# Reading the moving tile of every float32r product from its last column to its first

## Chip, cores and metric

One core of one Trainium2 chip. The metric is the device time in microseconds (us) of the kernel's one launch. The time of the kernel before is the median of three runs; a separate profiled execution gives the span, the busy times and the rows below.

## What is computed

One layer of a streaming-encoder trunk on a sequence of 1024 positions of width 1024, all in float32. The layer normalises its input, projects it, mixes it in four branches (chunked attention, a gated linear recurrence, a spatial gate, a recurrent branch with a convolution), projects and gates each branch, sums them, projects the sum and adds it to the input. A second half normalises again and applies a gated feed-forward network of hidden width 2816. Cut to what matters:

```python
def hybrid_mixer(h, w_in, ..., w_branch, w_out):
    z = h @ w_in
    aq, ak, av, bq, bf, bi, bg, cu, cv, dx, dg, gates = split_in(z)
    ...
    proj = jnp.einsum('bsnw,nwd->bsnd', outs, w_branch)
    g = jax.nn.sigmoid(gates.reshape(B, S, N_BRANCH, D_MODEL))
    merged = jnp.sum(g * proj, axis=2)
    return merged @ w_out

def swiglu(h, w1, w2):
    gt, up = jnp.split(h @ w1, 2, axis=-1)
    return (jax.nn.silu(gt) * up) @ w2

def reference(x, ...):
    h = rms_norm(x, norm_mix_pre[l])
    y = hybrid_mixer(h, ...)
    x = x + rms_norm(y, norm_mix_post[l])
    h = rms_norm(x, norm_ffn_pre[l])
    x = x + rms_norm(swiglu(h, w_ffn_in[l], w_ffn_out[l]), norm_ffn_post[l])
```

The large matrix products (with `w_in`, `w_branch`, `w_out`, `w_ffn_in`, `w_ffn_out`) are where almost all of TensorE's time goes.

## The kernel before, in words

Each large float32 product is made of three products of the faster type float32r. Both operands are split into a high part (a copy rounded to float32r, ScalarE, L135) and a low part (the rest, VectorE, L136). Then high times high, high times low and low times high are added up in one PSUM bank. A TensorE product takes a stationary operand of 128 rows and 128 columns, which a weight load brings in, and streams a moving tile of 128 rows and up to 512 columns past it. Each moving column gives one PSUM column.

The three products are issued in two places. `mm3` (L208 to L212) serves everything up to the feed-forward sums: the loop runs over the k tiles and issues L210, L211 and L212 for each, all into the same PSUM tile. `gemm_cm` calls it with weights stationary and 512 tokens moving, `gemm_tm` with tokens stationary and 256 weight columns moving, two groups of which fill one PSUM tile. `wino` (seven products of half-size blocks in place of eight, with sums of blocks made beforehand by `column_sums` and `token_sums`) calls it through its own `prod`. The local `step` of `ffn_out` (L1225 to L1230) issues the same three products for the last large multiplication, on units of which columns 0 to 511 are stationary and 512 to 1023 are moving.

Four steps of the order of work bear on the change. The tiles of PSUM come from one pool of eight banks, `pp` (L54): a new tile takes the bank of the tile that was released longest ago, so a product that opens a tile may have to wait for those who used the bank before. A tile framework records every dependency and puts semaphore waits on the instructions. A scheduler with a timeline model of its own sets the order in which each engine's instructions stand. And each finished tile is read once or twice from PSUM by ScalarE or VectorE in ascending column order (L340, L349, L356, L1072, L1262).

The small products of the branches (attention scores, transposes, the recurrences) are plain float32 and are issued elsewhere (L379, L541, L554, L666, L685, L698 and others). The diff does not touch them.

Of the kernel before, what the change touches and what calls it, by code (L numbers as in the profile page):

```python
# [38 lines left out]
def hybrid_trunk(ctx, tc, x, w_in, w_branch, w_out, w_ffn_in, w_ffn_out, cols, gpost, gfpost,  # L39
                 abias, wst, bsr, wabd, wxbd, lvl, tril, eye, out, dbg=None):  # L40
    nc = tc.nc
# [164 lines left out]

    def mm3(ps, lh, ll, rh, rl, n, more=False, ks=None):

        for k in ks or range(n):
            nc.tensor.matmul(ps, lhsT=lh(k), rhs=rh(k), start=(not more and k == 0), stop=False, skip_group_check=more)  # L210
            nc.tensor.matmul(ps, lhsT=lh(k), rhs=rl(k), start=False, stop=False, skip_group_check=more)  # L211
            nc.tensor.matmul(ps, lhsT=ll(k), rhs=rh(k), start=False, stop=(k == n - 1), skip_group_check=more)  # L212

    def gemm_cm(unit, xh, xl, fn, name, cs=slice(0, P), n=KT, fine=1):
        hi, lo = unit
        for h in range(2):
            ps = psmm(name)
            ts = slice(h * 512, (h + 1) * 512)
            for f in range(fine):
                mm3(ps, lambda k: hi[:, k, cs], lambda k: lo[:, k, cs],  # L220
                    lambda k: xh(k, ts), lambda k: xl(k, ts), n, ks=range(f * n // fine, (f + 1) * n // fine))
                if f == fine - 1:
                    fn(ps, ts)
                yield

    def gemm_tm(units, xh, xl, fn, name, tts):
        (ha, la), (hb, lb_) = units
        for tt in tts:
            ps = psmm(name)
            for u in range(2):  # L230
                ts = slice((tt + u) * P, (tt + u + 1) * P)
                mm3(ps[:, u * 256 : (u + 1) * 256], lambda k: xh(k, ts), lambda k: xl(k, ts),
                    lambda k: (ha if k < 4 else hb)[:, k % 4, :], lambda k: (la if k < 4 else lb_)[:, k % 4, :], KT)
            fn(ps, tt)
            yield
# [86 lines left out]
    def wino(ops, c0_, c1_, done):  # L322
# [11 lines left out]
        def prod(ps, un, o, b, more=False):  # L334
            mm3(ps, lambda k: un[0][:, o + k, :], lambda k: un[1][:, o + k, :], ops[b][0], ops[b][1], 4, more)
# [834 lines left out]
    def ffn_out(chunk, first, final):  # L1170
        n = len(chunk)
# [53 lines left out]
        def step(un, ps, t, start, stop, more):  # L1225
            hi, lo = un
            ts = slice(t * P, (t + 1) * P)
            nc.tensor.matmul(ps, lhsT=hi[:, ts], rhs=hi[:, 512:1024], start=start, stop=False, skip_group_check=more)  # L1228
            nc.tensor.matmul(ps, lhsT=hi[:, ts], rhs=lo[:, 512:1024], start=False, stop=False, skip_group_check=more)  # L1229
            nc.tensor.matmul(ps, lhsT=lo[:, ts], rhs=hi[:, 512:1024], start=False, stop=stop, skip_group_check=more)  # L1230

        n_prod = [0]

        def prod(pst, A, B, evac, more=False, after=None):

            n_prod[0] += 1
            if not final:
                for i, q in enumerate(pairs_):
                    u = units(q, A, B)
                    for t in range(4):  # L1240
                        step(u, pst[t], t, not more and i == 0, i == n - 1, more)
                        if i == n - 1:
                            evac(t, pst[t])
                    if after:
                        after(q)
                return

            un = [units(q, A, B, n_prod[0] in (2, 4, 6, 7)) for q in pairs_]
            for q in pairs_ if after else ():
                after(q)  # L1250
            for t in range(4):
                for i in range(n):
                    step(un[i], pst[t], t, not more and i == 0, i == n - 1, more)
                evac(t, pst[t])
# [133 lines left out]
```

## Time and profile before

| what | value |
|---|---|
| median of three runs | 1612.23 us (1610.47 to 1612.44) |
| profiled execution: its own time | 1611.69 us |
| profiled execution: span from first to last instruction | 1609.9 us |
| TensorE (PE) busy | 1535.5 us, 95% of the span |
| VectorE (DVE) busy | 1059.6 us, 66% |
| GpSimd (POOL) busy | 607.1 us, 38% |
| ScalarE (ACT) busy | 571.7 us, 36% |
| mean granted TensorE clock | 0.986 of 2.4 GHz |

In the profile a product stands as a MATMUL on PE and its weight load as an LDWEIGHTS on PEld, which overlaps PE. A product's duration runs from its start to the end of its passage through the array, so neighbours overlap: what a product costs in a dense stream is the distance between two starts, called its pitch here, and not its duration. The profiled execution took 1.8 us more than its span and lies 0.5 us below the median.

### The profile page before, as it was taken

How to read it: one execution, taken by the hardware profiler on the slowest of the kernel's cores; microseconds unless marked ns; L12 is line 12 of the kernel's file. 1: busy time of each engine (PE TensorE's matmuls, PEld its weight loads, DVE VectorE, ACT ScalarE, POOL GpSimd, SP SyncE). 2: the span in 40 equal slices, each digit the busy share in tenths (PEclk: the TensorE clock that was granted, in tenths of full speed). 3: DMA queues.
4: the chain of work that ended last, by engine and by line, in shares of the span. 5: the costliest groups of instructions: out<-in, count | busy, mean ns of one | idle time of the engine just before them, and what ended most of it. 6: DMA issues, size and time to landing. Idle time of an engine off the chain costs nothing. (4 is left out here: it accounts for less than half of the span.)

```text
span 1609.9 us, 20631 instructions
## 1 busy us (share of the span) xinstructions
PE 1535.5 (95%) x7880; PEld 1278.8 (79%) x7880; DVE 1059.6 (66%) x1415; ACT 571.7 (36%) x945; POOL 607.1 (38%) x475
## 2 busy tenths in 40 slices
PE   7899999999998999999999988999999999898986
PEld 7888888888887878776899966888888888686865
DVE  5986674444479475656766698555455556879898
ACT  6333343333322253334335533222232323343533
POOL 2665333323100101222442256533333335729194
PEclk9999999999999999999999998999999999999988
DMA  6224333333461148432325511222222236430212
GB/s 237 100 93 159 115 112 105 112 105 105 159 220 60 50 160 319 159 144 87 110 93 183 188 42 66 85 79 86 79 79 83 81 121 231 185 105 26 80 53 105
DMA packets 108547, 191.48 MB, mean 119 GB/s; under 512 B 6432, under 2 KB 65440, under 8 KB 108448
## 3 DMA queue, kind: packets, MB, share of 16 engines
q1 hardware_dynamic: 108448, 190.16, 33.9%
q8 instruction: 62, 1.02, 0.3%
q14 instruction: 37, 0.30, 0.1%
HBM read 136.66 MB, written 53.48 MB: 118 GB/s over the span
## 5 line engine op out<-in xcount | busy, mean ns | idle before, releaser
L136 DVE TENSOR_TENSOR wlo_ws<-s,whi_ws 128x1024 fp32r<-128x1024 f32 x78 | 118.2, 1515 | 51.8 <-ACT whi_ws L135 51.8
L356 DVE TENSOR_TENSOR u<-u,mm_w 128x512 f32<-128x512 f32 x39 | 26.8, 687 | 175.9 <-PE mm_w L212 175.9
L135 ACT CAST whi_ws<-s 128x1024 fp32r<-128x1024 f32 x78 | 82.2, 1054 | 157.4 <-PE mm_w L211 146.8
L1229 PE MATMUL mm_fo<-wlo_fo,whi_fo 128*128 128x512 f32 x308 | 123.7, 404 | 12.1 <-DVE wlo_fo L136 12.1
L319 POOL TENSOR_TENSOR s<-raw_pj 128x512 f32<-128x512 f32 x38 | 59.0, 1553 | 197.2 <-DMA raw_pj<-in_w_in 187.1
L1230 PE MATMUL mm_fo<-whi_fo,wlo_fo 128*128 128x512 f32 x308 | 119.4, 396 | 0.0
L319 POOL TENSOR_TENSOR s<-raw_fu 128x512 f32<-128x512 f32 x20 | 35.1, 1757 | 200.5 <-DMA raw_fu<-in_w_ffn_in 200.5
L1228 PE MATMUL mm_fo<-whi_fo 128*128 128x512 f32 x308 | 94.5, 399 | 9.3 <-ACT whi_fo L135 8.0
L136 DVE TENSOR_TENSOR wlo_fo<-af,whi_fo 128x512 fp32r<-128x512 f32 x66 | 72.9, 1112 | 26.3 <-ACT whi_fo L135 25.8
L1229 PEld LDWEIGHTS mm_fo<-wlo_fo,whi_fo 128*128 128x128 f32 x308 | 59.4, 193 | 30.7 <-DVE wlo_fo L136 18.4
L135 ACT CAST whi_fo<-af 128x512 fp32r<-128x512 f32 x66 | 40.6, 622 | 106.7 <-PE mm_fo L1230 56.0
L1228 PEld LDWEIGHTS mm_fo<-whi_fo 128*128 128x128 f32 x308 | 59.1, 192 | 23.7 <-ACT whi_fo L135 9.3
L340 ACT COPY m<-mm_w 128x512 f32<-128x512 f32 x39 | 22.9, 587 | 154.4 <-PE mm_w L212 140.7
L211 PE MATMUL mm_wo<-wlo_wo,mh 128*128 128x256 f32 x256 | 72.3, 284 | 1.9 <-DVE wlo_wo L136 1.9
L212 PE MATMUL mm_wo<-whi_wo,ml 128*128 128x256 f32 x256 | 72.4, 284 | 1.7 <-DVE ml L918 1.7
L210 PE MATMUL mm_w<-h2h,whi_wa 128*128 128x512 f32 x160 | 63.0, 394 | 10.9 <-ACT m L340 10.9
L210 PE MATMUL mm_wo<-whi_wo,mh 128*128 128x256 f32 x256 | 71.7, 284 | 0.7 <-ACT whi_wo L135 0.7
L1230 PEld LDWEIGHTS mm_fo<-whi_fo,wlo_fo 128*128 128x128 f32 x308 | 59.2, 192 | 12.1
L211 PE MATMUL mm_w<-h2l,whi_wa 128*128 128x512 f32 x160 | 62.7, 392 | 0.0
L212 PE MATMUL mm_w<-h2h,wlo_wa 128*128 128x512 f32 x160 | 62.7, 392 | 0.0
L210 PE MATMUL mm_w<-T2h,whi_ws 128*128 128x512 f32 x156 | 60.9, 390 | 0.6 <-ACT whi_ws L135 0.6
L212 PE MATMUL mm_w<-T4h,a 128*128 128x512 f32 x156 | 60.7, 389 | 0.0
(399 smaller groups left out, 4825.0 us busy)
## 6 DMA issues: line engine op xcount, KB each, us to landing
raw_pj<-in_w_in SPq DMA_DIRECT2D x19, 1024.0 KB, 6.0
gt<-st_g SPq DMA_DIRECT2D x22, 512.0 KB, 6.4
raw_fg<-in_w_ffn_in SPq DMA_DIRECT2D x11, 1024.0 KB, 4.9
raw_fu<-in_w_ffn_in SPq DMA_DIRECT2D x11, 1024.0 KB, 5.5
af<-act SPq DMA_DIRECT2D x22, 512.0 KB, 4.3
wf<-in_w_ffn_out SPq DMA_DIRECT2D x18, 512.0 KB, 6.6
xt<-in_x SPq DMA_DIRECT2D x16, 512.0 KB, 7.7
raw_wo<-in_w_out SPq DMA_DIRECT2D x8, 1024.0 KB, 5.1
```

The costliest lines, as they stand in the source:

```text
L135: nc.scalar.copy(hi, src)
L136: nc.vector.tensor_tensor(lo, src, hi.bitcast(F32), op=ALU.subtract)
L210: nc.tensor.matmul(ps, lhsT=lh(k), rhs=rh(k), start=(not more and k == 0), stop=False, skip_group_check=more)
L211: nc.tensor.matmul(ps, lhsT=lh(k), rhs=rl(k), start=False, stop=False, skip_group_check=more)
L212: nc.tensor.matmul(ps, lhsT=ll(k), rhs=rh(k), start=False, stop=(k == n - 1), skip_group_check=more)
L319: last_sum[0] = nc.gpsimd.tensor_tensor(out_, x0, x1_, op=op)
L340: nc.scalar.copy(m1, p1)
L356: nc.vector.tensor_tensor(u2, u2, p3, op=ALU.add)
L1228: nc.tensor.matmul(ps, lhsT=hi[:, ts], rhs=hi[:, 512:1024], start=start, stop=False, skip_group_check=more)
L1229: nc.tensor.matmul(ps, lhsT=hi[:, ts], rhs=lo[:, 512:1024], start=False, stop=False, skip_group_check=more)
L1230: nc.tensor.matmul(ps, lhsT=lo[:, ts], rhs=hi[:, 512:1024], start=False, stop=stop, skip_group_check=more)
```

## The change

In both places the moving tile and the PSUM tile are taken with their columns reversed (`[:, ::-1]`). The address of the first element is that of the last column, and the step along the row is -1 in place of +1, for what is read from SBUF and for what is written to PSUM alike. So column c of the moving tile still gives column c of PSUM, and the stationary operand is untouched.

```diff
     def mm3(ps, lh, ll, rh, rl, n, more=False, ks=None):
 
+        pd = ps[:, ::-1]
         for k in ks or range(n):
-            nc.tensor.matmul(ps, lhsT=lh(k), rhs=rh(k), start=(not more and k == 0), stop=False, skip_group_check=more)
-            nc.tensor.matmul(ps, lhsT=lh(k), rhs=rl(k), start=False, stop=False, skip_group_check=more)
-            nc.tensor.matmul(ps, lhsT=ll(k), rhs=rh(k), start=False, stop=(k == n - 1), skip_group_check=more)
+            h, l = rh(k)[:, ::-1], rl(k)[:, ::-1]
+            nc.tensor.matmul(pd, lhsT=lh(k), rhs=h, start=(not more and k == 0), stop=False, skip_group_check=more)
+            nc.tensor.matmul(pd, lhsT=lh(k), rhs=l, start=False, stop=False, skip_group_check=more)
+            nc.tensor.matmul(pd, lhsT=ll(k), rhs=h, start=False, stop=(k == n - 1), skip_group_check=more)
...
             ts = slice(t * P, (t + 1) * P)
-            nc.tensor.matmul(ps, lhsT=hi[:, ts], rhs=hi[:, 512:1024], start=start, stop=False, skip_group_check=more)
-            nc.tensor.matmul(ps, lhsT=hi[:, ts], rhs=lo[:, 512:1024], start=False, stop=False, skip_group_check=more)
-            nc.tensor.matmul(ps, lhsT=lo[:, ts], rhs=hi[:, 512:1024], start=False, stop=stop, skip_group_check=more)
+            pd, h, l = ps[:, ::-1], hi[:, 512:1024][:, ::-1], lo[:, 512:1024][:, ::-1]
+            nc.tensor.matmul(pd, lhsT=hi[:, ts], rhs=h, start=start, stop=False, skip_group_check=more)
+            nc.tensor.matmul(pd, lhsT=hi[:, ts], rhs=l, start=False, stop=False, skip_group_check=more)
+            nc.tensor.matmul(pd, lhsT=lo[:, ts], rhs=h, start=False, stop=stop, skip_group_check=more)
```

In the built program 6,600 products carry the step of -1: 5,256 of 512 columns and 1,344 of 256. Apart from line numbers (those of `mm3` grow by 2, those of `step` by 3), the instructions of all five engines stand in the same order in both programs. What differs are semaphore waits on PE. Two places follow; `[waits ...]` names the engines or queues whose count an instruction waits for.

PE in the first long run of `wino` products, at the product that opens the PSUM tile `mm_w_197` (with moving tile `T1h`) and at the end of the product before it; first the kernel before, then the change:

```order
L211 MATMUL mm_w_195_1514<-hTl_29_163,whi_wa_1498 128x512
L212 MATMUL mm_w_195_1514<-hTh_28_160,wlo_wa_1499 128x512
L210 MATMUL mm_w_197_1516<-T1h_735,whi_ws_191_1502 128x512
L211 MATMUL mm_w_197_1516<-T1l_736,whi_ws_191_1502 128x512
L212 MATMUL mm_w_197_1516<-T1h_735,wlo_ws_191_1503 128x512
```

```order
L213 MATMUL mm_w_195_1514<-hTl_29_163,whi_wa_1498 128x512
L214 MATMUL mm_w_195_1514<-hTh_28_160,wlo_wa_1499 128x512
L212 MATMUL mm_w_197_1516<-T1h_735,whi_ws_191_1502 128x512 [waits PE_49]
L213 MATMUL mm_w_197_1516<-T1l_736,whi_ws_191_1502 128x512
L214 MATMUL mm_w_197_1516<-T1h_735,wlo_ws_191_1503 128x512
```

The product that opens the tile now waits for PE's own count, that is for the end of an earlier product which wrote the same PSUM bank.

PE at the start of `ffn_out`, where the last `wino` product ends and the tiles `mm_fo_1672` and `mm_fo_1673` are opened; first before, then the change:

```order
L1228 MATMUL mm_fo_1672_10978<-whi_fo_10986 128x512 [waits Activation_49]
L1229 MATMUL mm_fo_1672_10978<-wlo_fo_10987,whi_fo_10986 128x512 [waits DVE_49]
L1230 MATMUL mm_fo_1672_10978<-whi_fo_10986,wlo_fo_10987 128x512
L1228 MATMUL mm_fo_1673_10979<-whi_fo_10986 128x512
L1229 MATMUL mm_fo_1673_10979<-wlo_fo_10987,whi_fo_10986 128x512
```

```order
L1231 MATMUL mm_fo_1672_10978<-whi_fo_10986 128x512 [waits PE_49,Activation_49]
L1232 MATMUL mm_fo_1672_10978<-wlo_fo_10987,whi_fo_10986 128x512 [waits DVE_49]
L1233 MATMUL mm_fo_1672_10978<-whi_fo_10986,wlo_fo_10987 128x512
L1231 MATMUL mm_fo_1673_10979<-whi_fo_10986 128x512 [waits PE_49]
L1232 MATMUL mm_fo_1673_10979<-wlo_fo_10987,whi_fo_10986 128x512
```

The same wait appears at each tile that is opened. Where a product waits for two counts, an instruction of its own on PE (EVENT_SEMAPHORE) holds one of them. In all, 210 instructions of PE wait for PE's own count in place of 93, and PE has 119 EVENT_SEMAPHORE instructions in place of 108. In the built program the product waited for by an added wait stands at least 24 products ahead of the waiting one, and in 37 cases 132 products ahead.

## Rows read from the trace of the kernel before

**Rows 1.** The page: span, busy time by engine, and the granted clock in 40 slices.

```profile
span 1609.9 us, 20631 instructions
PE 1535.5 (95%) x7880; PEld 1278.8 (79%) x7880; DVE 1059.6 (66%) x1415; ACT 571.7 (36%) x945; POOL 607.1 (38%) x475
PEclk9999999999999999999999998999999999999988
```

**Rows 2.** Busy time by stretch (stretch: length, PE busy, PEld, DVE, ACT, POOL, clock, DMA).

```profile
40.00:120.00 80.00, 72.44 (x507) 67.85 (x506) 73.26 (x117) 30.40 (x52) 51.72 (x30) 0.96 0.28 97
120.00:500.00 380.00, 377.33 (x1838) 313.10 (x1837) 213.29 (x286) 123.49 (x171) 108.95 (x71) 1.00 0.39 130
...
920.00:1000.00 80.00, 65.89 (x290) 54.20 (x289) 70.10 (x76) 29.13 (x51) 43.95 (x29) 0.91 0.20 70
1000.00:1380.00 380.00, 377.86 (x1662) 311.35 (x1660) 218.55 (x225) 111.34 (x155) 157.11 (x94) 1.00 0.32 110
...
1560.00:1609.90 49.90, 35.58 (x147) 28.31 (x146) 41.08 (x59) 16.32 (x38) 29.10 (x33) 0.88 0.34 127
```

**Rows 3.** Timeline of PE, products of 512 columns at 1300 us (start, duration).

```profile
1299.67 0.39 PE L212 MATMUL mm_w<-h2h,wlo_ws 128*128 128x512 f32 x1
...
1301.94 0.39 PE L212 MATMUL mm_w<-T2h,wlo_ws 128*128 128x512 f32 x1
1302.16 0.39 PE L210 MATMUL mm_w<-h2h,whi_wa 128*128 128x512 f32 x1
...
1303.98 0.39 PE L212 MATMUL mm_w<-h2h,wlo_wa 128*128 128x512 f32 x1
```

**Rows 4.** Timeline of PE, products of 256 columns at 850 us.

```profile
849.74 0.28 PE L212 MATMUL mm_wo<-whi_wo,ml 128*128 128x256 f32 x1
...
851.90 0.28 PE L212 MATMUL mm_wo<-whi_wo,ml 128*128 128x256 f32 x1
```

**Rows 5.** Timeline of PE after a wait of 10.91 us, products of 512 columns.

```profile
973.34 0.80 PE L210 MATMUL mm_w<-h2h,whi_wa 128*128 128x512 f32 x1 [10.91 <-ACT m L340]
973.93 0.63 PE L211 MATMUL mm_w<-h2l,whi_wa 128*128 128x512 f32 x1
...
975.64 0.63 PE L212 MATMUL mm_w<-h2h,wlo_wa 128*128 128x512 f32 x1
```

**Rows 6.** PE by stretch: length, busy time, granted clock, inside Rows 5 and just behind.

```profile
973.50:976.00 2.50, 2.50 (x6) 0.50 0.02 7
976.50:977.50 1.00, 1.00 (x6) 1.00 0.00 0
```

**Rows 7.** Timeline of PE at 103 us, where two products wait for PE's own count.

```profile
103.02 0.39 PE L211 MATMUL mm_w<-T2l,whi_ws 128*128 128x512 f32 x1
103.25 0.39 PE L210 MATMUL mm_w<-T1h,whi_ws 128*128 128x512 f32 x1
103.48 0.40 PE L211 MATMUL mm_w<-T1l,whi_ws 128*128 128x512 f32 x1
103.72 0.39 PE L210 MATMUL mm_w<-T4h,a 128*128 128x512 f32 x1
103.95 0.40 PE L211 MATMUL mm_w<-T4l,a 128*128 128x512 f32 x1
```

**Rows 8.** Line L210: its EVENT_SEMAPHORE instructions, and idle time before it put to issuing.

```profile
L210 PEldq EVENT_SEMAPHORE  x46: 51/51/51, 48.6 to 1342.3; - x46
...
  issue: 0.5, 2
```

**Rows 9.** The chain that ended last: first long piece and last piece.

```profile
1589.21 1.51 POOL ya L1273
...
1606.17 0.66 DVE x1b L1287
```

## The prediction

> **What bounds the kernel now.** I read the page first, then the busy time by stretch, then the timeline of TensorE. The reader is to see on the page that PE is busy for 1535.5 us of a span of 1609.9 us, at a granted clock of nearly full speed throughout [rows 1]. An engine that is busy for 95% of the time sets the end, unless its idle time hides something. The stretches say where that holds: from 120 to 500 us and from 1000 to 1380 us PE works for 377.33 and 377.86 of 380 us, with VectorE far below it. Only from 40 to 120 us, from 920 to 1000 us and after 1560 us is VectorE busier than PE [rows 2]. The chain that ended last covers just the tail, from 1589 us, on POOL and VectorE [rows 9]. All of PE's idle time together is 1609.9 - 1535.5 = 74.4 us. So a lasting change of what a product costs goes into the time almost one for one, and that cost has to be read from starts, not from durations. At 1300 us twenty products of 512 columns start between 1299.67 and 1303.98 us, so their pitch is 4.31 / 19 = 0.227 us, though each has a duration of 0.39 us [rows 3]. Nineteen products of 256 columns start between 849.74 and 851.90 us: 2.16 / 18 = 0.120 us [rows 4]. The difference, 0.227 - 0.120 = 0.107 us for 256 columns, is 0.417 ns a column, which is one column per cycle of 2.4 GHz. What is left of the pitch, 0.227 - 512 x 0.000417 = 0.0135 us, is a fixed part of each product, the same in both forms. At the lower clock it does not show: after the wait of 10.91 us the granted clock is 0.50, that is 1.2 GHz [rows 6], and the products from 973.93 to 975.64 us have a pitch of 1.71 / 4 = 0.4275 us, 0.835 ns a column, with nothing left over [rows 5].
>
> **The change, part by part.** 5,256 products of 512 columns and 1,344 of 256 run backwards: 5,256 x 512 + 1,344 x 256 = 3,035,136 columns. At the pitches above they take 5,256 x 0.227 + 1,344 x 0.120 = 1,354 us, most of what PE does. The order of the instructions stays what it was on every engine, no operand is moved, and no transfer is added or removed. So there are three terms.
>
> First, the stream itself. Nothing in the trace before streams with a step of -1, so I bound it. It can cost nothing: each address is still one element from the last, the same elements share every small block of memory, and the array takes one column a cycle from wherever it comes. It can cost a full second cycle per column, if reader or writer takes two neighbours at once only in ascending order: 3,035,136 x 0.417 ns = 1,266 us. The nearest row for a stream at half rate is the one at 1.2 GHz, with 0.4275 us for 512 columns [rows 5]; it shows that the rest of the kernel bears such a pitch without further harm, not that a step of -1 causes it. Below zero it can go only by the fixed part, 6,600 x 0.0135 = 89 us; that part does not depend on the number of columns, and a change of the order of columns gives no reason for it to go. I take zero, because the quantity that moves data here, an element beside the last one each cycle, is unchanged; both ends stay for the range.
>
> Second, the waits. 117 more instructions of PE wait for PE's own count. The product waited for stands at least 24 products ahead, and even at the smaller pitch that is 24 x 0.120 = 2.9 us, while a product has left the array 0.39 us after its start [rows 3]. So the wait is always over when it is reached, and what it can cost is handling. The trace before has such waits: at 103 us the first products with T1h and with T4h wait for PE's count, and start 0.23 and 0.24 us after their predecessors [rows 7], at most 0.013 us above the pitch. The neighbours without a wait stand 0.23 us apart as well. Bounds: 0 and 117 x 0.013 = 1.5 us; I take 0.5 us, a third of the upper end, since one of the two rows keeps the pitch. Queued behind each waiting product are only PE's own next weight loads, which are covered, and whoever reads the tile waits for its last product, not its first.
>
> Third, 11 more EVENT_SEMAPHORE instructions on PE. Of those before, 46 stand in the stream of L210 at 51 ns each, and the idle time put to issuing before that line is 0.5 us in two cases [rows 8]. They run while earlier products are still in the array. Without that cover they would cost 11 x 0.051 = 0.6 us; I take 0.
>
> The readers of PSUM (L340, L349, L356, L1072, L1262) begin after a tile's last product, so it does not matter to them which column came last. The sum: 0 + 0.5 + 0 = 0.5 us on the profiled execution's own 1611.7 us, 1612.2 us; that execution lies 0.5 us below the median, so I put the new median at 1612.7 us. A measurement of this kernel can tell about 0.2%, 3.2 us, from no change.
>
> **The rivals.**
>
> *Half rate.* If two neighbouring columns are only handled together when their addresses ascend, each product takes one column per two cycles. PE's time grows by 1,266 us; at best all of its 74.4 us of idle time, much of it waiting for VectorE, is filled, so 1,192 to 1,266 us and 2,804 to 2,878 us in all. For it speaks that a stream of one float32 column per cycle of 2.4 GHz [rows 3, 4] leaves little slack, and that no row shows it with another step; against it, that neighbours stay neighbours in either direction, and that 512 and 256 are even, so that no pair of columns is split. I give it 0.16. The Trainium skill points this way: "PSUM — Partial Sum Buffer" (Specifications) gives lines of 8 bytes and says that any non-contiguous pattern slows matmuls significantly. Taken by the letter, a step of -1 is not contiguous and the sum would be 1,266 us. The same rule in "Advanced Engine Details and Errata" (PSUM Cachelines) asks that every two consecutive elements be contiguous, which 511 and 510 are, and by that the sum stays at 0.5 us. No row of this case decides between the two readings.
>
> *A larger fixed part.* The fixed 0.0135 us is paid where one product follows the other, and there the address jumps by a row's length, forward now where it was backward. If this made it longer, up to twice, the time would rise by up to 89 us, to 1,701 us. For it: the part exists and its cause is not in the trace. Against it: it is the same for jumps of 256 and of 512 columns, so the jump's size at least does not enter. 0.06.
>
> *The waits hold the weight load.* If a product that waits for PE's count kept the next weight load from overlapping, PE would have to let the product before it run out: its duration less its pitch, 0.39 - 0.227 = 0.163 us [rows 3], 117 times, 19 us, 1,631 us. It decides from 3.2 / 117 = 0.027 us for each wait. Against it stand the two waits at 103 us with at most 0.013 us. 0.06.
>
> *Faster.* The fixed part shrinks or goes, down to 1,524 us. Nothing speaks for it but that its cause is unknown. 0.04.
>
> That the program undoes the reversal is excluded: the built products carry the step of -1.
>
> **How the numbers follow.** No change has 0.68, the half rate 0.16, the larger fixed part 0.06, the waits 0.06, faster 0.04. The predicted time is that of the likeliest, 1612.7 us. The range goes from 1608 us (0.2% below and a little of what three runs scatter) to 1702 us, the end of the fixed part; this takes in the first, third and fourth case, 0.68 + 0.06 + 0.06 = 0.80, and leaves out the half rate and the gain. Slower by over 0.2%: 0.16 + 0.06 + 0.06 = 0.28. Within 0.2%: 0.68. Faster by over 0.2%: 0.04.
>
> **What would show it.** Right: the pitch of 512 columns is again 0.227 us and that of 256 again 0.120 us; PE's busy time stays within a few us of 1535 us; the product that opens a tile starts one pitch after its predecessor, with a wait for PE's count or without. Wrong: a pitch near 0.44 us for 512 columns and 0.227 us for 256 at a granted clock of 1.00 (half rate); equal added amounts on both forms, such as 0.24 and 0.133 us (the fixed part); or gaps before the opening products alone (the waits). A pitch that grows in only one of the two forms would be none of these.

## The result and the profile after

The change made the kernel slower: 1639.4 us against 1611.35 us for the kernel before, each the median of four runs taken side by side, a ratio of 1.0173 with a 95% interval of 1.0156 to 1.0191. That is 28.05 us more. It lies inside the range of the prediction and outside its forecast of no change; the likeliest case was wrong.

The page of the changed kernel, span, busy times and clock, to be held against [rows 1]:

```profile
span 1638.2 us, 20642 instructions
PE 1568.4 (96%) x7880; PEld 1283.7 (78%) x7880; DVE 1059.8 (65%) x1415; ACT 571.1 (35%) x945; POOL 598.8 (37%) x475
PEclk9999999999999999999999998999999999999998
```

The number of products is what it was, and the clock and the work of the other engines nearly so (GpSimd's busy time is 8.3 us lower). PE is busy for 32.9 us longer (1568.4 - 1535.5), and its idle time falls from 74.4 to 1638.2 - 1568.4 = 69.8 us. The span grows by the difference, 28.3 us. The loss is therefore in the products, and about a seventh of it is covered by idle time that was there before.

The timeline of PE in the changed kernel in a dense stretch of products of 512 columns (start, duration); 177 products start from the first row to the last without a break:

```profile
1289.73 0.40 PE L212 MATMUL mm_w<-h2h,whi_wa 128*128 128x512 f32 x1
...
1329.86 0.40 PE L213 MATMUL mm_w<-h2l,whi_wa 128*128 128x512 f32 x1
1330.10 0.40 PE L214 MATMUL mm_w<-h2h,wlo_wa 128*128 128x512 f32 x1
1330.33 0.40 PE L212 MATMUL mm_w<-T1h,whi_ws 128*128 128x512 f32 x1
1330.56 0.40 PE L213 MATMUL mm_w<-T1l,whi_ws 128*128 128x512 f32 x1
1330.80 0.40 PE L214 MATMUL mm_w<-T1h,wlo_ws 128*128 128x512 f32 x1
```

The pitch is 41.07 / 176 = 0.2333 us, against 0.227 us in [rows 3]: 6.5 ns more for each product. The product with T1h at 1330.33 us is one that opens a PSUM tile and now waits for PE's own count; it stands 0.23 us after its predecessor, like all others. The waits have left no gap.

The products of 256 columns, the same view, 20 products, against [rows 4]:

```profile
864.72 0.28 PE L214 MATMUL mm_wo<-whi_wo,ml 128*128 128x256 f32 x1
...
866.97 0.28 PE L212 MATMUL mm_wo<-whi_wo,mh 128*128 128x256 f32 x1
```

Their pitch is 2.25 / 19 = 0.1184 us, a little shorter than the 0.120 us before. And at the lower clock, where [rows 5] had 0.4275 us for 512 columns, seven products after a wait:

```profile
989.84 0.63 PE L213 MATMUL mm_w<-h2l,whi_wa 128*128 128x512 f32 x1
...
992.39 0.63 PE L213 MATMUL mm_w<-h2l,whi_wa 128*128 128x512 f32 x1
```

2.55 / 6 = 0.425 us, the same within the 0.01 us to which starts are given: there the change costs nothing. So at 2.4 GHz the two forms move apart, 5,256 x 6.5 ns = +34.2 us and 1,344 x -1.6 ns = -2.2 us, together 32.0 us, and PE's busy time shows 32.9.

### The profile page after: what moved, and what is told of

It is laid out like the page before. It is cut to its first block, busy times and chain, and to the rows that moved or that the text cites. A ratio compares the mean times of both kernels' runs of the same rounds, so it can differ in the third digit from the quotient of the medians.

```text
span 1638.2 us, 20642 instructions
## 1 busy us (share of the span) xinstructions
PE 1568.4 (96%) x7880; PEld 1283.7 (78%) x7880; DVE 1059.8 (65%) x1415; ACT 571.1 (35%) x945; POOL 598.8 (37%) x475
## 5 line engine op out<-in xcount | busy, mean ns | idle before, releaser
L321 POOL TENSOR_TENSOR s<-raw_pj 128x512 f32<-128x512 f32 x38 | 63.8, 1678 | 206.3 <-DMA raw_pj<-in_w_in 184.2
L321 POOL TENSOR_TENSOR s<-raw_fu 128x512 f32<-128x512 f32 x20 | 30.9, 1547 | 212.1 <-DMA raw_fu<-in_w_ffn_in 212.1
L214 PE MATMUL mm_w<-T2h,wlo_ws 128*128 128x512 f32 x156 | 62.1, 398 | 0.0
```

The costliest lines, as they stand in the source:

```text
L214: nc.tensor.matmul(pd, lhsT=ll(k), rhs=h, start=False, stop=(k == n - 1), skip_group_check=more)
L321: last_sum[0] = nc.gpsimd.tensor_tensor(out_, x0, x1_, op=op)
```

## The experiments

Two kinds of kernel were used. Five are the change's kernel with an edit, timed against the kernel before (e1 to e5). Four are streams alone (m1 to m4): no layer, only runs of 32 or 48 float32r products (in m1 also bfloat16) into one PSUM tile each, one form after another, with the other engines all but idle. Each of the four ran once; streams that stand in two of them agree within 0.04 us of some 7.5. Three theories are named in what was expected: R, that the descending read costs; W, that the descending write does; N, that either costs only beside the other engines' traffic. The core of the streams is this, with `rd` giving the moving tile's order, `wr` PSUM's, and in m3 and m4 the weights' first column varied as well (there the weights go through six places, not eight):

```python
for k in range(reps):
    nc.tensor.matmul(wr(ps, k), lhsT=w[:, (k % 8) * P : (k % 8 + 1) * P], rhs=rd(m, k),
                     start=(k == 0), stop=(k == reps - 1), skip_group_check=True)
```

In their rows the timeline gives each stream as one line: start, length, tile, shape, and the number of products. The pitch follows as the length less one product's duration (0.39 to 0.40 us for 512 columns, 0.28 for 256, 0.34 for 384), divided by one less than the number. The ratios of e1 to e5 are to runs of the kernel before beside them (median 1610.44 us for e1 to e3, 1610.12 us for e4 and e5).

**e1: only the read descends.** In both places PSUM is written in ascending order.

```diff
-        pd = ps[:, ::-1]
+        pd = ps
...
-            pd, h, l = ps[:, ::-1], hi[:, 512:1024][:, ::-1], lo[:, 512:1024][:, ::-1]
+            pd, h, l = ps, hi[:, 512:1024][:, ::-1], lo[:, 512:1024][:, ::-1]
```

> Only the read descends; PSUM is written in ascending order, so each product's columns come out mirrored. This program has no more waits on PE's own count than the kernel before (93). Theory R: 1.017 times the time before, the pitch of 512 columns 0.2333 us. Theory W and the theory that the 117 waits cost it: 1.000, pitch 0.2267 us.

Measured: 1639.5 us, ratio 1.0182 (1.0168 to 1.0196). Its page:

```profile
span 1638.5 us, 20631 instructions
PE 1569.1 (96%) x7880; PEld 1281.4 (78%) x7880; DVE 1060.2 (65%) x1415; ACT 571.1 (35%) x945; POOL 599.9 (37%) x475
```

The whole loss is there, without a single added wait (the program has 20,631 instructions, as before).

**e2: only the write descends.**

```diff
-            h, l = rh(k)[:, ::-1], rl(k)[:, ::-1]
+            h, l = rh(k), rl(k)
...
-            pd, h, l = ps[:, ::-1], hi[:, 512:1024][:, ::-1], lo[:, 512:1024][:, ::-1]
+            pd, h, l = ps[:, ::-1], hi[:, 512:1024], lo[:, 512:1024]
```

> Only the write descends; the moving tile is read in ascending order, so each product's columns come out mirrored. This program has all of the change's waits (210 instructions of PE wait for PE's own count). Theory R: 1.000 to 1.001 times the time before, which is then also the price of the waits. Theory W: 1.017, pitch of 512 columns 0.2333 us. Theory of the waits: 1.017 with a pitch of 0.2267 us and gaps at the products that open a tile.

Measured: 1610.34 us, ratio 1.0001 (0.9991 to 1.0010).

```profile
span 1609.0 us, 20642 instructions
PE 1534.3 (95%) x7880; PEld 1277.6 (79%) x7880; DVE 1061.8 (66%) x1415; ACT 571.5 (36%) x945; POOL 606.5 (38%) x475
```

PE's busy time is back at 1534.3 us, though all 20,642 instructions with the added waits are there. The descending write and the waits cost nothing that can be measured, at most 0.001 x 1610 = 1.6 us together. Theory R holds in the kernel; theory W and the waits fall.

**m1: the four combinations as streams alone, and other lengths.**

> A kernel of streams alone: each stream is 48 products into one PSUM tile, with nothing else running beside it; the names tell how the moving tile is read and how PSUM is written (f ascending, r descending: rf512x reads descending and writes ascending) and the columns. It leaves out all of the layer's computation. Theory R (the descending read from SBUF costs): rr512x and rf512x have a pitch of 0.2333 us, ff512x and fr512x one of 0.2267. Theory W (the descending write to PSUM costs): rr512x and fr512x 0.2333, ff512x and rf512x 0.2267. Theory N (only beside the other engines' traffic does it cost): all four forms of 512 columns 0.2267. If the cost is a rate per column, as 0.2333 us for 512 columns and about 0.1184 for 256 in the change's own trace suggest (0.449 ns a column and 3 ns fixed), 384 descending columns take 0.176 us and 128 about 0.061, if the weight load allows it; if it is a fixed part, 384 and 128 columns are each longer by the same amount as 512. Ascending: 0.417 ns a column and 0.0134 us, so 0.1734 us for 384. Two descending halves and thirty-two descending runs of 16 should behave as 512 descending if the step decides, and as ascending if the start at the top of the tile does.

The timeline of PE; the two letters of a name stand for read and write, f ascending and r descending, so rf is a descending read with an ascending write:

```profile
22.62 10.82 PE L52 MATMUL ff512x<-mv,wt 128*128 128x512 f32 x47
44.24 11.37 PE L52 MATMUL rf512x<-mv,wt 128*128 128x512 f32 x48
55.44 11.06 PE L52 MATMUL fr512x<-mv,wt 128*128 128x512 f32 x48
66.34 5.92 PE L52 MATMUL ff256x<-mv,wt 128*128 128x256 f32 x48
77.78 5.84 PE L52 MATMUL rf256x<-mv,wt 128*128 128x256 f32 x48
89.21 8.49 PE L52 MATMUL ff384x<-mv,wt 128*128 128x384 f32 x48
106.06 8.70 PE L52 MATMUL rf384x<-mv,wt 128*128 128x384 f32 x48
166.62 12.96 PE L52 MATMUL sixteenx<-mv,wt 128*128 128x512 f32 x48
179.42 11.54 PE L52 MATMUL ffodd<-mv,wt 128*128 128x512 f32 x48
202.10 11.20 PE L52 MATMUL rstep<-mv,wt 128*128 128x256 f32 x48
213.12 10.55 PE L52 MATMUL wstep<-mvb,wtb 128*128 128x256 bf16 x48
233.88 10.52 PE L52 MATMUL brrx<-mvb,wtb 128*128 128x512 bf16 x47
244.24 5.41 PE L52 MATMUL bffs<-mvb,wtb 128*128 128x256 bf16 x48
```

Of 512 columns the descending read takes (11.37 - 0.40) / 47 = 0.2334 us, the descending write (11.06 - 0.39) / 47 = 0.2270 us, and both ascending (10.82 - 0.39) / 46 = 0.2267 us: theory R again, and not N, as nothing else runs here. For 384 columns it is 0.178 against 0.173 us, for 256 columns 0.1183 against 0.1200 us. So the loss is neither the same for each product nor the same for each column. Two other rows were not foreseen by any theory: an ascending read that starts one column later (ffodd) takes 0.237 us, more than the descending one, and thirty-two descending runs of 16 (sixteenx) take 0.267 us. For 128 columns 0.061 us was expected, if the weight load allowed it; all four forms take about 0.11 us (5.47 to 5.52 us for 48), and no order shows. By an estimate that is the weight load: in m3 a load of 128 columns lasts 0.188 us and one of 32 columns 0.108 us, 0.83 ns a column, so 0.107 us for 128. In bfloat16 descending read and write together cost nothing: 48 products, of which the trace has 47, at (10.52 - 0.38) / 47 = 0.2157 us, and 0.216 us between neighbouring starts ascending. It had been expected that two descending halves (halfx) would tell step from start; they take 0.2334 us like the whole, which does not decide it.

Two streams of 256 columns with a step of 2 show what the step of -1 does not do. Read with a step of 2, a float32r product takes about 0.23 us (rstep, 11.20 us for 48), nearly twice the 0.120 us of ff256x; written with a step of 2, a bfloat16 product has 10.55 us in its stream where step 1 has 5.41 (wstep, bffs). So something close to the half rate that the prediction weighed does exist, for elements that are not neighbours.

**e3: only the products of 256 columns run backwards.**

```diff
+        back = ps.shape[-1] == 256
-        pd = ps[:, ::-1]
+        pd = ps[:, ::-1] if back else ps
...
-            h, l = rh(k)[:, ::-1], rl(k)[:, ::-1]
+            h, l = (rh(k)[:, ::-1], rl(k)[:, ::-1]) if back else (rh(k), rl(k))
```

> Only the 1,344 products of 256 columns run backwards, in read and write; those of 512 columns are as before. If the trace of the change is read rightly, their pitch falls from 0.120 to about 0.1184 us, 1,344 x 1.6 ns = 2.1 us in all, so 0.9987 to 1.000 times the time before. If the products of 256 columns share in the loss, 1.001 or more.

Measured: 1610.06 us, ratio 0.9997 (0.9988 to 1.0006). PE's busy time is 1532.8 us, 2.7 us below that of the kernel before:

```profile
span 1607.8 us, 20634 instructions
PE 1532.8 (95%) x7880; PEld 1276.7 (79%) x7880; DVE 1063.8 (66%) x1415; ACT 571.3 (36%) x945; POOL 607.0 (38%) x475
```

The timeline of PE shows the pitch itself, 27 products of 256 columns:

```profile
848.78 0.28 PE L213 MATMUL mm_wo<-whi_wo,mh 128*128 128x256 f32 x1
...
851.86 0.28 PE L215 MATMUL mm_wo<-whi_wo,ml 128*128 128x256 f32 x1
```

3.08 / 26 = 0.1185 us, as expected. The busy time alone would not show it, as e4 below has 1532.7 us without a shorter pitch. In the kernel's time a gain of 2 us cannot be told from no change by these runs. It is the only version that the experiments point to as better than both kernels, and it is not shown to be.

**m2: which part of the order costs.**

> Streams alone again, 32 products of 512 columns each, all writing PSUM in ascending order; the layer's computation is left out. Names: f or r and a letter for the first column of the moving tile (a = 0, b = 1, c = 2, d = 3, e = 4, g = 6, i = 8, m = 12, p = 15, q = 16, G = 32), read ascending (f) or descending (r); and blocks of 2, 4, 8, 16, 64 or 128 columns read with the blocks descending and each block ascending (down), or the blocks ascending and each block descending (in). Theory L (it costs that successive lines of 16 bytes, four columns, go down): fourdown 0.2333 us as for all descending, fourin 0.2267 as for all ascending. Theory I (it costs that neighbours inside a line go down): fourin 0.2333 or more, fourdown 0.2267. Theory A (only the address of the first element counts, relative to some block of memory): the descending stream reaches 0.2267 us at one of the starts, and the ascending one shows 0.2333 or more at others; rising starts then repeat with a period of 4, 8, 16 or 32 columns. If every change of direction at a block's end costs, both block forms grow with the number of blocks, by about 4 cycles a block of 16 (0.267 us) as measured before.

```profile
69.40 7.83 PE L52 MATMUL rdo<-mv,wt 128*128 128x512 f32 x32
166.24 7.61 PE L52 MATMUL fGo<-mv,wt 128*128 128x512 f32 x32
196.00 7.63 PE L52 MATMUL fourdown<-mv,wt 128*128 128x512 f32 x32
203.47 7.43 PE L52 MATMUL fourin<-mv,wt 128*128 128x512 f32 x32
218.21 7.63 PE L52 MATMUL eightin<-mv,wt 128*128 128x512 f32 x32
225.67 7.63 PE L52 MATMUL sixteendown<-mv,wt 128*128 128x512 f32 x32
233.14 8.69 PE L52 MATMUL sixteenin<-mv,wt 128*128 128x512 f32 x32
241.67 7.43 PE L52 MATMUL sixtyfourdown<-mv,wt 128*128 128x512 f32 x32
```

A stream of 32 products takes 7.43 us where the pitch is 0.227 us, and 7.63 us where it is 0.233 us. Turned inside blocks of four columns, the step of -1 costs nothing (fourin); with blocks of four descending and each one ascending, the whole loss is there (fourdown). Theory I falls, and theory L, that it costs when successive lines of 16 bytes go down, foresaw both. Theory L alone does not tell all. The loss does not grow with the number of lines that go down: it is the same where every second step between lines goes down (eightin) and where only every fourth does (sixteendown). Blocks of 64 in descending order cost nothing (sixtyfourdown), blocks of 16 that descend inside cost 0.267 us (sixteenin), and ascending streams that start elsewhere lose as well (fGo, from column 32, 7.61 us). Not every shifted start costs: one from column 15 (fpo) takes 7.42 us. None of the descending streams, at eleven starts, had a pitch under 0.233 us; the dearest (rdo, from column 3) took 7.83. So theory A falls for the descending read and holds in part for the ascending one.

**e4 and e5: two of these orders in the whole kernel.** With c=4 blocks ascend and the columns of each descend; with c=64 the blocks descend and their columns ascend. Read and write alike go through `turned`.

```diff
+    def turned(a):
+        return a.rearrange("p (b c) -> p b c", c=4)[:, :, ::-1]
...
+    def turned(a):
+        return a.rearrange("p (b c) -> p b c", c=64)[:, ::-1, :]
```

> The change's kernel, but each product's columns turned only inside blocks of four (16 bytes): in read and write alike, blocks ascend and the four columns of each descend, so results are in place. All of the change's waits are there (210). Theory L (successive lines of 16 bytes in descending order cost): 1.000 times the time before, pitch of 512 columns 0.2267 us. If the step of -1 itself costs: 1.017.

> The change's kernel, but with blocks of 64 columns (256 bytes) in descending order and ascending columns in each, in read and write alike: each product still starts near the top of its tile and ends near the bottom. From the stream of this order alone: 0.2267 us for 512 columns, 1.000 times the time before. If the direction in which a product passes over its tile, or where it hands over to the next one, costs: 1.017.

Measured: e4 1610.35 us, ratio 0.9998 (0.9988 to 1.0007), e5 1609.96 us, ratio 1.0000 (0.9991 to 1.0009). PE is busy for 1532.7 and 1534.9 us. In both traces two neighbouring starts in dense runs of 512 columns are 0.227 us apart on average, as in the kernel before; in the changed kernel 0.233. Neither a step of -1 by itself, nor starting at the top and ending at the bottom of a tile, costs anything that can be measured in the kernel.

**m3: the weight load beside the stream.** Shifting the weights' first column leaves the moving tile where it is.

> Streams alone, 32 products of 512 columns each, PSUM written ascending; the layer's computation is left out. Moving tiles are read ascending (names ending in f) or descending (r) from their first column. What varies is the weight load beside it: its first column shifted by 0, 4, 8, 16, 32 or 64 columns (wzero, wfour, weight, wsixteen, wthirty, wsixty), one and the same weight tile every time (same), or 64 or 32 columns of weights instead of 128 (half, thirty). Theory K (what costs is that the moving read and the weight load, which run at the same time, meet in the same blocks of SBUF): shifting the weights changes the pitch of the ascending stream, up to 0.233 us and more, or brings the descending one down to 0.2267 us at some shift, and with 32 columns of weights the difference between f and r goes. Theory O (the moving read alone, whatever is loaded): f 0.2267 and r 0.2333 us at every shift and at every width.

```profile
48.04 7.62 PE L50 MATMUL weightf<-mv,wt 128*128 128x512 f32 x32
55.50 7.63 PE L50 MATMUL weightr<-mv,wt 128*128 128x512 f32 x32
62.97 7.63 PE L50 MATMUL wsixteenf<-mv,wt 128*128 128x512 f32 x32
92.82 7.46 PE L50 MATMUL wsixtyf<-mv,wt 128*128 128x512 f32 x32
107.58 7.43 PE L50 MATMUL samef<-mv,wt 128*128 128x512 f32 x32
137.15 7.57 PE L50 MATMUL thirtyf<-mv,wt 128*32 128x512 f32 x32
144.56 7.63 PE L50 MATMUL thirtyr<-mv,wt 128*32 128x512 f32 x32
```

An ascending stream whose moving tile has not moved loses as much as a descending one once its weights start 8 or 16 columns later (weightf, wsixteenf; 7.64 us at 4 and 7.61 at 32), and recovers at 64 (wsixtyf). So theory O falls for the ascending read. The descending stream has its 0.233 us a product with every weight tile, and also with weight loads of 32 columns, which last 0.108 us in place of 0.188. So for the descending read theory O is not refuted. One expectation of theory K was missed: with 32 columns of weights the two directions do not meet at the good value; the ascending stream rises instead (7.57 against 7.63 us), which theory K does not explain.

**m4: both shifted.**

> Streams alone, 32 products of 512 columns each, the layer's computation left out. Ascending streams with the first column shifted in the moving tile alone (mv), in the weight tile alone (wt) or by the same amount in both (both), by 1, 2, 3, 4, 8, 16, 32 and 64 columns; then descending streams (rev) with the weight tile shifted by 1, 2, 3, 12, 48 and 96 columns. Theory K (the moving read and the weight load meet in SBUF, and what counts is where they stand to each other): an ascending stream with both shifted alike keeps 0.2267 us or comes near it, while one shifted alone costs up to 0.2333 and more; a descending stream, for which they never stand the same way twice, keeps 0.2333 us at all six. Theory S (each of the two reads pays for its own start, whatever the other does): both shifted costs at least as much as the dearer of the two alone.

```profile
86.64 7.56 PE L50 MATMUL fourboth<-mv,wt 128*128 128x512 f32 x32
101.44 7.62 PE L50 MATMUL fourwt<-mv,wt 128*128 128x512 f32 x32
108.90 7.45 PE L50 MATMUL eightboth<-mv,wt 128*128 128x512 f32 x32
116.19 7.62 PE L50 MATMUL eightmv<-mv,wt 128*128 128x512 f32 x32
123.65 7.63 PE L50 MATMUL eightwt<-mv,wt 128*128 128x512 f32 x32
131.12 7.42 PE L50 MATMUL sixteenboth<-mv,wt 128*128 128x512 f32 x32
138.38 7.49 PE L50 MATMUL sixteenmv<-mv,wt 128*128 128x512 f32 x32
145.70 7.62 PE L50 MATMUL sixteenwt<-mv,wt 128*128 128x512 f32 x32
234.46 7.63 PE L50 MATMUL ninetyrev<-mv,wt 128*128 128x512 f32 x32
```

Shifted by 8, one of the two alone costs 7.62 or 7.63 us, both together 7.45; by 16 it is 7.49 and 7.62 alone and 7.42 together. At 32 columns the picture is the same (7.61 and 7.60 alone, 7.44 together). At these shifts it is their place relative to each other that counts, as theory K says, and theory S falls there. Below 8 columns this is not so: shifted by 4, both together take 7.56 us, and shifted by 1 they are the dearest of all (0.238 us a product; 0.237 for the moving tile alone, 0.232 for the weights alone). All six descending streams take 7.63 us, ninetyrev standing for them.

## Why the prediction was wrong in its likeliest case

**What bounds the kernel** was right: a change of the pitch went into the time, 28.3 of 32.9 us, and the pitch was the place to look.

**The first term failed.** The prediction put the stream at zero "because the quantity that moves data here, an element beside the last one each cycle, is unchanged". It measured +6.5 ns for each product of 512 columns and -1.6 ns for each of 256, 32 us in place of 0. The reasoning took "an element beside the last one" to be all that a read's cost depends on. What e1 and e2 show is that the descending read from SBUF carries the whole cost; m2, e4 and e5 show that it comes when lines of 16 bytes, or blocks of up to 16 columns, are taken in descending order, not from the step of -1 and not with blocks of 64. m3 and m4 show that an ascending read's pitch depends also on where the weight load beside it stands. That the descending read's loss has to do with the weight load is not shown: no shift, width or repetition of the weights changed it. The kernel before had the good case in its dense runs, moving tiles and weights both starting at multiples of 128 columns of their tiles, and its pitch of 0.227 us is the shortest that any stream of 512 float32r columns here reached. The bounds held (0 and 1,266 us), but were too far apart to help.

**The waits** were right in kind: expected 0.5 us, measured as no more than 1.6 us together with the descending write (e2), and no gap in the trace at the product that opens a tile. The event instructions likewise.

**The rivals.** The half rate did not happen; its signature, 0.44 us for 512 columns at full clock, is absent; a step of 2 would have shown something like it (rstep, wstep in m1), a step of -1 does not. The reading of "PSUM — Partial Sum Buffer" (the Trainium skill, Specifications) by which any pattern that is not contiguous slows matmuls does not hold for a descending write of unit step: e2 has 1.0001. The larger fixed part came nearest in size, being the only rival whose range of 0 to 89 us holds the 28 us, but it was to add the same amount to both forms, and the products of 256 columns became shorter. None of the rivals named the mechanism. The prediction had said that a pitch that grows in only one of the two forms would be none of these, and that is what came.

**The numbers.** 1639.4 us lies in the range of 1608 to 1702 us. "Slower" had 0.28, and within 0.2%, which had 0.68, was the wrong favourite. That the result lies in the range is luck: its upper end came from a longer fixed part, which did not happen. That this part of 0.0135 us had no known cause was the hint that the pitch is not only columns and clock.

What stays open: why a descending read of 512 columns takes 0.233 us whatever the weights' place, and why one of 256 gets shorter. Since the weight load is a read too, its direction may matter, and a descending stationary operand was not tried. That the two reads meet in the same part of SBUF, even for the ascending read, is inferred from the shifts; no row shows it.

## What to carry to other kernels

Judge a matmul's operand order by its pitch in a dense run, in each form that the kernel uses, since durations, busy shares and bfloat16 experience do not show a few nanoseconds in a float32r product. For float32r keep the moving tile in ascending order, at least line by line, and start it and the weights at multiples of 64 columns of their tiles; equal shifts of 8, 16 and 32 columns kept the good pitch in the streams, equal shifts of 1 to 4 did not. To mirror something, turn the columns on the PSUM side, where it was free. That no instruction moves does not make a reordered operand free: multiply a possible few nanoseconds by the number of products before calling it nothing.

## What was not expected of the hardware

The streams' own floors differ by type: 512 columns take 0.2157 us in bfloat16 and 0.227 us at best in float32r, at the same granted clock. The direction moves only the latter; the starting columns moved it too (0.227 to 0.240 us in all), and were not varied in bfloat16.

A float32r product's pitch at 2.4 GHz depends on the first column of the weight tile: with the moving tile unchanged, weights 16 columns later cost 7.63 in place of 7.43 us in 32 products. "TensorE: Matmul & The Clock Gate" (the Trainium skill, Part 2, the step on LDWEIGHTS) says that loading the next tile's weights takes no SBUF read bandwidth from the running matmul. These float32r streams do not fit that: each product took 6.5 ns longer when only the weights' place changed. How the load gets in the way is not shown, and for bfloat16 no run here varied the weights' place.

At 1.2 GHz the descending order cost nothing (0.425 us for 512 columns against 0.4275 us before).
